# Scores one unit ahead of the attention, and seven pairs of query tiles by seven products instead of four

## The chip, the cores and the metric

The kernel runs on one core of a Trainium2 chip. The metric is the device time of one execution in microseconds (us); before the change it is 1146.06 us, the median of three runs (1145.57 to 1146.4). TensorE (PE in the profile) multiplies matrices, VectorE (DVE), ScalarE (ACT) and GpSimd (POOL) do elementwise work, and SyncE (SP) issues most DMAs. Each engine works through its own instructions in order.

## The reference, cut to what matters

Two layers on a sequence of 1024 positions with 1024 features, all in float32. The first is gated linear attention. The second, which the change touches, attends with eight query heads to one shared set of keys and values, in three groups of dilated windows (dilations 1, 4 and 16). It mixes the groups by their log-sum-exp, gates the result and projects it.

```python
q = rope(q.reshape(bsz, s, SWA_N_GROUPS * SWA_Q_HEADS, SWA_HEAD_DIM), pos) * (SWA_HEAD_DIM ** -0.5)
q = q.reshape(bsz, s, SWA_N_GROUPS, SWA_Q_HEADS, SWA_HEAD_DIM)
outs, lses = [], []
for gi, (window, dilation) in enumerate(SWA_GROUPS):
    o_g, lse_g = dilated_window_attention(q[:, :, gi], k_sh[:, :, gi], v_sh[:, :, gi], window, dilation)
    outs.append(o_g)
    lses.append(lse_g)
wts = jax.nn.softmax(jnp.stack(lses, axis=0), axis=0)
o = jnp.sum(wts[..., None] * jnp.stack(outs, axis=0), axis=0)
return (o.reshape(bsz, s, SWA_OUT).astype(x.dtype) * jax.nn.silu(g)) @ w_out
```

## The kernel before, in words

The program records its operations and then orders them itself: `Sched.order` (lines 263 to 405) is a list scheduler. Each operation has a cost from a table, `cost` (564 to 616), and a rank, the place where it was recorded, shifted by `S.later`. For each engine the scheduler takes, among the operations whose inputs and buffers are there, the one that can start first by these costs, and among equals the one recorded first. For TensorE an operand that comes from another engine counts 0.35 us later than it is expected (`AHEAD`). So the code's order of writing and the costs set the static order on each engine. All instructions are issued from line 462, which is why the profile names groups by tile and not by line.

Float32 products are made of three fast matmuls: high by high, high by low, low by high. The activations of the second layer lie in SBUF as `x1h` and `x1l`, the weights as `wh` and `wl`.

A unit is one query head with its three groups. For unit u, `q_proj` (1439) makes three query tiles of 128 features by 1024 positions: plain projections of 2 halves by 8 k-tiles by 3 matmuls into a bank `acc`, then a rotation (`rope`, 1227) on DVE, ACT and POOL. `g_proj` (1449) is a projection of the same size for the gate. `scores` (1466) multiplies Q by the keys in fp32 into two banks `lv`, takes the row minimum and the mask on DVE (statistics `sts` and `nat`), the exponential and its sum on ACT (tile `P`), then sends the statistics through DRAM (`std`, `nat<-std`), forms the weights of the groups on DVE (`cw`, `ew`) and sends these through DRAM too (`cwd`, `cw<-cwd`). `attend` (1552) scales P by the weights, makes the product of group 2 over a diagonal layout (`diag`, banks `po`), transposes P on TensorE (banks `ms`), forms `PT` on DVE and POOL, multiplies PT by V into `po` and adds into `og`.

Before the attention stands a stage in which pairs of 128-column tiles are projected by seven products instead of eight (`seven`, 1292): from sums of halves of the weights and of the activations (`T1` to `T4`, 16 pages). A product is 4 k-tiles by 3 matmuls of 512 columns. Its sums and combinations are extra passes on DVE, ACT and POOL. The three pairs of key tiles go this way, and the pairs of query tiles in the list `EARLY` (line 40), each entry two units and a group. These are rotated, stored to DRAM (`qd`) and loaded again by `q_proj` when their unit is due.

The loop of the attention (1646 to 1665) is: scores of u, gate of u-1, queries of u+1, attend of u. So projections of the units around stand between the scores and the attend of a unit. For unit 4 the keys and values change: `reload_k(1)` and `reload_v(1)` are recorded to wait for unit 3's weights (`S.behind(cwd[3])`). A pool of 16 pages `pg` holds K and V (three each), Q (three per unit) and part of P; smaller tiles share 13 buffers `a`.

Of the kernel before, what the change touches and what calls it, by code (L numbers as in the profile page):

```python
# [36 lines left out]
AHEAD = 0.35  # L37
RUNS, GATHER = 0.3, 1.0
QUEUED, ISSUE, ADDED = 2.4, 0.9, 1.7
EARLY = [(0, 1, 2), (2, 3, 2), (4, 5, 2), (6, 7, 2)]  # L40


class Buf:
# [100 lines left out]
class Sched:  # L144
# [21 lines left out]
    def record(self, engs, meth, args, kw):  # L166
# [17 lines left out]
        elif meth == "activation":  # L184
            func = str(a[2]).split(".")[-1]
        costs = [cost(e, meth, n, outs, ins, args, kw) + self.extra for e in engs]
        g = self.group_op
        if g is None:
# [355 lines left out]
def jump(v):  # L544

    i = v.idx.reshape(-1) if v.idx.ndim == 1 else v.idx[(0,) * 1]
    while i.ndim > 1 and i.shape[-1] == 1:
        i = i[..., 0]
    i = i.reshape(-1, i.shape[-1])[0] if i.ndim > 1 else i
    return int(abs(i[1] - i[0])) * SIZE[v.buf.dtype] if len(i) > 1 else 0  # L550
# [13 lines left out]
def cost(e, meth, n, outs, ins, args, kw):  # L564

    if e == "PE":
        if meth == "transpose":
            return 0.07
        n = int(_np.prod(outs[0].shape[1:]))
        fast = "float32r" in str(args[2].dtype)  # L570
        if fast:
            return n / 2400 + 0.0135 if n >= 256 else 0.215
        if n >= 128:
            return 4 * n / 2400 + 0.009
        if args[1].shape[0] == 64:
            return 0.12
        m = args[1].shape[1]
        return {32: 0.02, 64: 0.05}.get(m, 0.43)
    if meth == "dma_start":
        return 0.1 + int(_np.prod((outs + ins)[0].shape)) * 4 / 280e3  # L580
    psum = any(v.buf.pool.space == "PSUM" for v in ins)
    pointers = sum(isinstance(kw.get(k), View) for k in ("bias", "scale")) + 2 * (meth == "affine") + (meth == "scale")
    if e == "ACT":
        c = 0.105 + n * 0.83e-3 + 0.093 * pointers - 0.04 * psum
        if outs[0].dtype == U16:
            c += 0.09
        return c + (0.1 if "accum_out" in kw else 0)
    step = jump(outs[0]) if not psum or meth != "matmul" else 0
    if e == "DVE":
        if meth == "reciprocal":  # L590
            return 0.07 + n * 6e-3
        c = 0.07 + n / 960.0
        if meth in ("scalar_tensor_tensor", "tensor_tensor_reduce"):
            c += 0.06
        if meth in ("tensor_tensor", "tensor_mul", "tensor_add", "tensor_sub") and psum:
            c += 0.1
        if meth == "scalar_tensor_tensor" and psum:
            c += 0.05
        if meth == "tensor_tensor_scan":
            c += n / 960.0  # L600
        if meth in ("tensor_scalar", "scale") and not psum:
            c = 0.17 + n * 0.36e-3
        if meth == "affine":
            c = 0.2 + n * 0.52e-3
        if outs[0].dtype == U16:
            c += 0.04
        if step >= 2048 // 4 * 2:
            c += 0.75e-3 * n
        elif step >= 512:
            c += 2.2e-3 * n  # L610
        elif step >= 32 and n >= 256:
            c += 0.75e-3 * n
        return c + (0.085 if "accum_out" in kw else 0)
    if meth in ("tensor_scalar", "affine", "scale"):
        return 0.3 + n * 0.65e-3
    return 0.1 + n * 2.35e-3


def trunk(tc, xT, wP, wA, wA12, wAv3, w2, wO, wK, wV0, wV12, wB, wOB, par_d,
          ident_d, lmask_d, cos_d, sin_d, bmask_d, rmask_d, tri_d, lnr_d, out):  # L620
    S = Sched(tc, lat=LAT, pad=PAD)
# [18 lines left out]
    def page(pool, dt, name):  # L640
        return pool.tile([128, T], dt, name=name, tag="pg", bufs=16)
# [4 lines left out]
    def hs(half):  # L646
        return slice(half * 512, half * 512 + 512)
# [36 lines left out]
    def project(piece, xs, evac, halves=(0, 1), added=False):  # L684
        w = load_w(piece, added)
        for half in halves:
            acc = ps.tile([128, 512], F32, name="acc", bufs=2)
            proj_cols(w, xs, hs(half), acc)
            with S.later(-EVAC):
                evac(half, acc)  # L690
# [393 lines left out]
    def small(name, tag, bufs, dt=F32, shape=(128, 512)):  # L1084
        return hp.tile(list(shape), dt, name=name, tag=tag, bufs=bufs)
# [100 lines left out]
    vd0 = [dram.tile([128, T], F32, name=f"vd0{c}") for c in range(2)]  # L1186
    qd = {(u, g): dram.tile([128, T], F32, name=f"qd{u}{g}") for *us, g in EARLY for u in us}

# [4 lines left out]
    cwd = [dram.tile([2, T], F32, name=f"cwd{k}") for k in range(NK)]  # L1193
# [15 lines left out]
    def layer_b(xs, early):  # L1209
# [17 lines left out]
        def rope(pg, g, half, acc):  # L1227
            r = hs(half)
            t1 = small("t1", "t1", 2)
            S.vector.tensor_mul(t1, acc, cosT[:, r])  # L1230
            t2 = small("t2", "t2", 2)
            S.scalar.copy(t2[0:64, :], acc[64:128, :])
            S.scalar.copy(t2[64:128, :], acc[0:64, :])
            S.vp.tensor_mul(t2, t2, sinT[:, r])
            S.vp.tensor_add(to_group(pg, g, half), tok_view(t1, g), tok_view(t2, g))
# [141 lines left out]
        def load_v(c, g):  # L1377
            V[c][g] = page(p0, F32, f"V{c}{g}")
            if g == 1:
                for n in range(2):  # L1380
                    S.sync.dma_start(
                        V[c][g].rearrange("p (r n e) -> p r n e", r=4, n=2)[:, :, n, :],
                        vd[n * 512:n * 512 + 512, c * 128:c * 128 + 128].rearrange("(p r) e -> p r e", r=4))
            else:

                src = vd3[c].rearrange("(n a s k j) e -> k s a n (j e)", n=8, a=8, s=2, k=2)
                for k in range(2):
                    for s in range(2):
                        S.sync.dma_start(V[c][g][k * 64:k * 64 + 64, s * 512:s * 512 + 512], src[k, s])

        def sigmoid_gate(sg, acc):
            th = small("th", "t1", 2)
            S.scalar.activation(th, acc, AF.Tanh, scale=0.5)
            S.vector.scalar_tensor_tensor(sg, th, 1.0, acc, op0=OP.add, op1=OP.mult)
# [7 lines left out]
        jobs = [((wK[2 * g], kd[0][g]), (wK[2 * g + 1], kd[1][g]), g) for g in range(3)]  # L1402
        jobs += [((wB[u, g], qd[u, g]), (wB[v, g], qd[v, g]), g) for u, v, g in EARLY]
        w = load_pair([a[0] for a in jobs[0][:2]], True)
# [9 lines left out]
        def reload_k(c):  # L1414
            for g in (2, 1, 0):
                K[c][g] = page(p0, F32, f"K{c}{g}")
                S.sync.dma_start(K[c][g], kd[c][g])

        def reload_v(c):
            load_v(c, 2)  # L1420
            load_v(c, 1)
            V[c][0] = page(p0, F32, f"V{c}0")
            S.sync.dma_start(V[c][0], vd0[c])
# [15 lines left out]
        def q_proj(u):  # L1439
            Q = [page(p0, F32, "Q") for _ in range(3)]  # L1440
            U[u]["Q"] = Q
            for g in range(3):
                if (u, g) in qd:
                    S.sync.dma_start(Q[g], qd[u, g])
                else:
                    project(wB[u, g], xs, lambda half, acc: rope(Q[g], g, half, acc), added=True)


        def g_proj(u):
            og = U[u]["og"]  # L1450

            def evac(half, acc):
                sg, r = small("sg", "t2", 2), hs(half)
                sigmoid_gate(sg, acc)
                S.vector.scalar_tensor_tensor(og[:, r], og[:, r], 0.5, sg, op0=OP.mult, op1=OP.mult)
                if u < 6:
                    S.sync.dma_start(ogB[u][:, r], og[:, r])
            project(wB[u, 3], xs, evac, added=True)
# [184 lines left out]
            S.vp.memset(x, 0.0)  # L1643
        q_proj(0)
        reload_v(0)
        for u in range(8):
            scores(u)
            if 0 < u < 5:
                g_proj(u - 1)
            if u == 3:  # L1650
                with S.behind(cwd[3]):
                    reload_k(1)
            if u + 1 < 8:
                q_proj(u + 1)
            if u < 7:
                attend(u)
            if u == 3:
                with S.behind(cwd[3]):
                    reload_v(1)
        for u in (4, 5, 6):  # L1660
            g_proj(u)
        early()
# [59 lines left out]
    def early():  # L1722
        ogs.clear()
        for half in range(2):
            for kt in range(4):
                with S.later(-EVAC):
                    load_og(ogB[kt], kt, p0, lambda: small("ogf", "a", 13), (half,))

    U = layer_b(x1s, early)
    for half in range(2):  # L1730
        for kt in range(4, 6):
# [116 lines left out]
```

## Time and profile before

| what | value |
|---|---|
| median of 3 runs | 1146.06 us |
| profiled execution | 1145.4 us |
| its span | 1143.6 us |
| mean granted TensorE clock | 0.998 |
| busy, PE / DVE / ACT / POOL | 1129.4 / 813.4 / 583.9 / 181.7 us |
| seven-product stage | from about 511 to 640 us |
| attention, first score to last attend | from 664 to 1047 us |

The span is the time from the first to the last instruction; the profiled execution has 1.8 us around it. Matmul records overlap, since matmuls are pipelined: a 512-column matmul has a record of about 0.39 us, while the next starts 0.23 us later. So a mean of matmul records is not the price of one more matmul; the distance between starts is. "Idle before" names the engine or DMA that ended a wait. "PEld" is the loading of weights into TensorE, which runs beside the matmuls.

### The profile page before, as it was taken

The numbers are of one execution on the slowest core, as the hardware profiler recorded it, in microseconds if no ns is written. First come the engines' busy times: TensorE is split into PE (matmuls) and PEld (weight loads), VectorE is DVE, ScalarE is ACT, GpSimd is POOL, SyncE is SP. The second block draws the span as 40 slices with busy tenths as digits, with TensorE's granted clock in tenths as the row PEclk, the third lists the DMA queues.
The fourth block names the chain that finished last, engine by engine and source line by source line (L and its number), as shares of the span: only waits on it lengthen the run. The fifth ranks groups of instructions, "written<-read, shape, count | busy, mean of one in ns | idle before, by whom it ended". The sixth has DMA issues, their size and how long they took to land.

```text
span 1143.6 us, 20006 instructions
## 1 busy us (share of the span) xinstructions
PE 1129.4 (99%) x7696; PEld 959.8 (84%) x7696; DVE 813.4 (71%) x1634; ACT 583.9 (51%) x1165; POOL 181.7 (16%) x168
## 2 busy tenths in 40 slices
PE   9999999999999999999999999999999999999997
PEld 9888888889987888887888878888878888888886
DVE  6286963686967599988989556676656667587578
ACT  5355531545563345656566467355545655643242
POOL 1000000100222111022232212022120122133000
PEclk9999999999999999999999999999999999999999
DMA  8111122211253453865566863444273433462545
GB/s 270 59 39 38 64 85 74 93 57 38 75 173 113 138 169 135 283 200 133 136 176 164 235 152 77 94 84 99 59 177 86 93 81 71 97 146 77 171 143 180
DMA packets 104031, 138.29 MB, mean 121 GB/s; under 512 B 44833, under 2 KB 63137, under 8 KB 103937
## 3 DMA queue, kind: packets, MB, share of 16 engines
q1 hardware_dynamic: 97888, 119.72, 34.2%
q0 software_dynamic: 6048, 17.30, 8.6%
q8 instruction: 60, 0.98, 0.3%
q14 instruction: 35, 0.28, 0.1%
HBM read 109.53 MB, written 27.46 MB: 120 GB/s over the span
## 4 chain that ended last, share of the span: by engine, by line
PE 89%; DVE 7%; ACT 1%; DMA 1%; issue 1%; SPq 0%; DVEq 0%; ACTq 0%
PE acc L462 47%; PE sev L462 11%; PE lv L462 9%; PE po L462 9%; PE vac L462 7%; PE ms L462 4%; PE pro L462 2%; DVE rt L462 2%; DVE wl L462 1%; DMA nat<-std 1%; DVE x1l L462 1%; DVE t L462 1%; DVE P L462 1%; ACT t L462 0%; DVE Q L462 0%
## 5 line engine op out<-in xcount | busy, mean ns | idle before, releaser
L462 ACT ACTIVATE wh<-wf 128x1024 fp32r<-128x1024 f32 (+3 forms) x111 | 106.4, 960 | 158.3 <-PE acc L462 118.3
L462 PE MATMUL acc<-x1h,wh 128*128 128x512 f32 x384 | 165.6, 431 | 1.0 <-ACT t L462 1.0
L462 PE MATMUL acc<-x1h,wl 128*128 128x512 f32 x384 | 150.6, 392 | 0.0
L462 PE MATMUL acc<-x1l,wh 128*128 128x512 f32 x384 | 150.0, 391 | 0.0
L462 DVE TENSOR_TENSOR wl<-wf,wh 128x1024 fp32r<-128x1024 f32 (+3 forms) x62 | 76.7, 1237 | 43.9 <-ACT wh L462 33.7
L462 PE MATMUL acc<-xh,wh 128*128 128x512 f32 x256 | 102.1, 399 | 0.0
L462 PE MATMUL acc<-xh,wl 128*128 128x512 f32 x256 | 99.9, 390 | 0.0
L462 PE MATMUL acc<-xl,wh 128*128 128x512 f32 x256 | 99.9, 390 | 0.0
L462 ACT ACTIVATE P<-P,sts 128x256 f32<-128x256 f32 (+1 forms) x128 | 59.9, 469 | 65.9 <-DVE sts L462 65.3
L462 PEld LDWEIGHTS acc<-x1h,wl 128*128 128x128 f32 x384 | 72.1, 188 | 15.9
L462 PEld LDWEIGHTS acc<-x1h,wh 128*128 128x128 f32 x384 | 72.6, 189 | 13.0 <-ACT t L462 1.2
L462 PEld LDWEIGHTS acc<-x1l,wh 128*128 128x128 f32 x384 | 72.6, 189 | 12.0
L462 PE MATMUL lv<-K,Q 128*64 128x64 f32 (+2 forms) x512 | 71.1, 288 | 0.9 <-DVE sts L462 0.8
L462 PE MATMUL sev<-T,wh 128*128 128x512 f32 x224 | 69.3, 391 | 0.1
L462 POOL DMA_DIRECT2D wl<-in_wB x36 | 31.8, 903 | 225.6 <-ACT wl L462 177.3
L462 DVE CUSTOM_DVE_ANT_0 P<-lv,bmask 128x256 f32<-128x256 f32 (+1 forms) x128 | 46.2, 378 | 27.4 <-PE lv L462 26.8
L462 PEld LDWEIGHTS lv<-K,Q 128*128 128x128 f32 (+1 forms) x512 | 53.8, 164 | 12.6 <-DVE sts L462 2.6
L462 PE MATMUL acc<-ogh,wh 128*128 128x512 f32 x152 | 60.3, 397 | 0.1
L462 PE MATMUL acc<-ogl,wh 128*128 128x512 f32 x152 | 59.4, 391 | 0.2 <-POOL ogl L462 0.2
L462 PE MATMUL acc<-ogh,wl 128*128 128x512 f32 x152 | 59.3, 390 | 0.0
L462 DVE TENSOR_TENSOR t<-t,sinT 128x512 f32<-128x512 f32 x46 | 34.4, 748 | 33.7 <-ACT t L462 33.6
L462 POOL TENSOR_TENSOR wl<-wf,wh 128x1024 fp32r<-128x1024 f32 x8 | 19.1, 2386 | 240.3 <-PE ms L462 145.5
(298 smaller groups left out, 2839.1 us busy)
## 6 DMA issues: line engine op xcount, KB each, us to landing
wf<-in_wB SPq DMA_DIRECT2D x32, 512.0 KB
wf<-in_wA SPq DMA_DIRECT2D x24, 512.0 KB
wl<-in_wB POOLq DMA_DIRECT2D x24, 512.0 KB, 7.9
wf<-in_wO SPq DMA_DIRECT2D x16, 512.0 KB
wf<-in_wOB SPq DMA_DIRECT2D x16, 512.0 KB
wf<-in_wV SPq DMA_DIRECT2D x12, 512.0 KB
res<-in_xT SPq DMA_DIRECT2D x16, 256.0 KB
x1d<-rt SPq DMA_DIRECT2D x16, 256.0 KB
```

The lines of the kernel that those rows point to most:

```text
L462: getattr(handle[o.eng], meth)(*[conv(a) for a in args], **{k: conv(v) for k, v in kw.items()})
```

## The change

`EARLY` gets three more entries: the group-1 query tiles of units 1 and 3, of 4 and 5, and of 6 and 7 are made as pairs by seven products before the attention, and stored to DRAM. Only group 0 of every unit, and group 1 of units 0 and 2, are still projected inside the attention. The table's cost of a transpose on TensorE goes from 0.07 to 0.11, which can move instructions everywhere in the program.

The loop is rewritten: scores of unit 0 and queries of unit 1 come first; then, for each u, scores of u+1, gate of u-1, queries of u+2, attend of u. So the P tiles of two units are held at once. The keys of the second half are loaded ahead of the scores of unit 4, still behind unit 3's weights; its values are no longer held behind those.

```diff
-EARLY = [(0, 1, 2), (2, 3, 2), (4, 5, 2), (6, 7, 2)]
+EARLY = [(0, 1, 2), (2, 3, 2), (1, 3, 1), (4, 5, 2), (6, 7, 2), (4, 5, 1), (6, 7, 1)]
...
         if meth == "transpose":
-            return 0.07
+            return 0.11
...
-        for u in range(8):
-            scores(u)
-            if 0 < u < 5:
-                g_proj(u - 1)
+        scores(0)
+        q_proj(1)
+        for u in range(7):
             if u == 3:
                 with S.behind(cwd[3]):
                     reload_k(1)
-            if u + 1 < 8:
-                q_proj(u + 1)
-            if u < 7:
-                attend(u)
+            scores(u + 1)
+            if 0 < u < 5:
+                g_proj(u - 1)
+            if u + 2 < 8:
+                q_proj(u + 2)
+            attend(u)
             if u == 3:
-                with S.behind(cwd[3]):
-                    reload_v(1)
+                reload_v(1)
```

## The prediction

> **What bounds the kernel now.** First the page: one engine fills the span.
>
> ```profile
> span 1143.6 us, 20006 instructions
> PE 1129.4 (99%) x7696; PEld 959.8 (84%) x7696; DVE 813.4 (71%) x1634; ACT 583.9 (51%) x1165; POOL 181.7 (16%) x168
> ```
>
> TensorE shows 99%, and the next engine, VectorE, 71%. Then the windows, for the two stages that the change touches: the seven-product stage, and the attention from the first score matmul to the last attend.
>
> ```profile
> 664.15:1047.00 382.85, 379.08 (x2273) 324.71 (x2273) 255.78 (x806) 214.74 (x616) 79.95 (x89) 1.00 0.44 96
> 518.00:640.00 122.00, 121.82 (x537) 100.96 (x538) 103.08 (x142) 75.16 (x126) 36.57 (x34) 1.00 0.63 168
> ```
>
> The columns behind the length are PE, PEld, DVE, ACT, POOL, then the granted clock and the DMA share. PE idles 382.85 - 379.08 = 3.8 us in the attention and 0.2 us in the other. So in both the time is the PE's work, and a matmul less is its slot less, as long as the other engines keep up. How long a slot is stands in the chain that ended last:
>
> ```profile
> 518.18 122.24 PE sev L462 x538
> 640.42 23.80 PE acc L462 x105
> ```
>
> 122.24/538 = 0.2272 us for a 512-column matmul of the seven-product stage, 23.80/105 = 0.2267 us for one of a plain projection.
>
> **Part 1: fewer matmuls.** A plain query tile costs 2 halves x 8 k-tiles x 3 = 96/2 = 48 matmuls, a pair 96. By seven products a pair costs 7 x 4 x 3 = 84. Three more pairs: 3 x 12 = 36 matmuls fewer, 36 x 0.227 = **-8.2 us**. The rest of a pair's price is on other engines (four sums, their splits, five combining adds, about 13 passes on DVE or POOL); at 103.08 of 122.00 us DVE has room in that stage, and three more pairs repeat the same mix, so this costs nothing. Without that cover it would cost what DVE needs beyond PE, and DVE needs 0.85 of it. The group-1 store of a rotated half has a strided output, but so have those of the K pairs and group-2 pairs that run there already:
>
> ```profile
> L462 DVE TENSOR_TENSOR pair<-t,t 128x512 f32<-128x512 f32 x28 | 29.4, 1049 | 2.4 <-DMA qd<-pair 1.2 <-POOL t L462 0.5
> qd<-pair SPq DMA_DIRECT2D x8, 512.0 KB
> wl<-in_wB POOLq DMA_DIRECT2D x24, 512.0 KB, 7.9
> ```
>
> On the queues, six 512 KB reads with add on POOL's queue become nine of 256 KB, and SP gets six more 512 KB stores to qd and six more loads of Q. At a DMA share of 0.63 and 0.44 these lie beside PE work: nothing.
>
> **Part 2: fewer changes of kind.** In the attention, projection matmuls are pushed between fp32 matmuls (scores, transposes, P times V). Here is what a change costs on PE (start, length):
>
> ```profile
> 670.35 0.38 PE L462 MATMUL lv<-K,Q 128*128 128x128 f32 x2
> 670.49 0.48 PE L462 MATMUL acc<-x1h,wh 128*128 128x512 f32 x1
> 670.80 0.40 PE L462 MATMUL acc<-x1l,wh 128*128 128x512 f32 x1
> 671.03 0.40 PE L462 MATMUL acc<-x1h,wl 128*128 128x512 f32 x1
> 671.27 0.59 PE L462 MATMUL lv<-K,Q 128*128 128x256 f32 x2
> 671.51 0.58 PE L462 MATMUL acc<-x1h,wh 128*128 128x512 f32 x1
> 671.93 0.40 PE L462 MATMUL acc<-x1l,wh 128*128 128x512 f32 x1
> ```
>
> The first projection matmul behind a score takes 0.31 and 0.42 us to the next start instead of 0.23. Over the kernel, the matmul that stands first in each group of three is longer than the second:
>
> ```profile
> L462 PE MATMUL acc<-x1h,wh 128*128 128x512 f32 x384 | 165.6, 431 | 1.0 <-ACT t L462 1.0
> L462 PE MATMUL acc<-x1l,wh 128*128 128x512 f32 x384 | 150.0, 391 | 0.0
> ```
>
> 165.6 - 150.0 = 15.6 us. The order of before has 121 such changes in the attention, that of after 106: 15.6/121 = 0.129 us each, 15 x 0.129 = **-1.9 us**. Both ends: nothing, if the longer matmuls come from another cause, and -1.9.
>
> **Part 3: waits in the attention.** The projection matmuls that fill it fall from 1047 to 756, and the order there changes. TensorE, unit 2's diagonal product in before (po<-diag is the group-2 product, ms the transposes of P, lv the next scores):
>
> ```order
> L462 MATMUL acc<-x1h_4386,wh 128x512
> L462 MATMUL acc<-x1l_4399,wh 128x512
> L462 MATMUL acc<-x1h_4386,wl 128x512
> L462 MATMUL acc<-x1h_4412,wh 128x512
> L462 MATMUL acc<-x1l_4426,wh 128x512
> L462 MATMUL acc<-x1h_4412,wl 128x512
> L462 MATMUL po<-diag,V_6513 128x128 x8
> L462 MATMUL acc<-x1h_4437,wh 128x512
> L462 MATMUL acc<-x1l_4452,wh 128x512
> L462 MATMUL acc<-x1h_4437,wl 128x512
> L462 MATMUL lv<-K_6281,Q 128x256
> ```
>
> TensorE in after, attend(1) into scores(3):
>
> ```order
> L462 MATMUL acc<-x1h_4335,wl 128x512
> L462 MATMUL ms<-ident,P 128x128 x4
> L462 MATMUL po<-diag,V_7020 128x128 x8
> L462 MATMUL ms<-ident,P 128x128 x8
> L462 MATMUL lv<-K_6780,Q 64x64 x16
> L462 MATMUL po<-PT,V_7027 128x128 x12
> L462 MATMUL po<-PT,V_7033 128x128
> L462 MATMUL lv<-K_6788,Q 128x128
> L462 MATMUL acc<-x1h_4366,wh 128x512
> L462 MATMUL acc<-x1l_4377,wh 128x512
> L462 MATMUL acc<-x1h_4366,wl 128x512
> L462 MATMUL po<-PT,V_7033 128x128 x14
> ```
>
> The attend now runs as one block with almost no projection between its steps. Before has one bare place of this kind, and it waits (timeline of PE; the bracket is the idle time ahead):
>
> ```profile
> 842.44 0.60 PE L462 MATMUL ms<-ident,P 128*128 128x128 f32 x4
> 844.08 2.21 PE L462 MATMUL po<-diag,V 128*128 128x128 f32 x16 [1.04 <-DVE diag L462]
> 847.32 0.51 PE L462 MATMUL acc<-x1h,wh 128*128 128x512 f32 x1 [1.03 <-ACT t L462]
> ```
>
> 1.04 + 1.03 = 2.07 us. In after the diagonal product is not so bare: in attend(1) eight transposes and twelve projections precede the four shown, the first four being its own. I take one such double wait more, +2.1; the ends are -3.8 (all idle gone) and seven times 2.07.
>
> The second place is on VectorE, whose in-order queue holds the reduction that waits for a unit's gathered statistics (cw<-nat). In before it stands among the rotations of the next Q:
>
> ```order
> L462 TENSOR_TENSOR Q<-t_7654,t_7656 128x512
> L462 TENSOR_TENSOR t_7701<-acc,cosT 128x512
> L462 TENSOR_REDUCE cw<-nat 128x8
> L462 TENSOR_TENSOR ew<-cw,nat 128x24
> L462 TENSOR_TENSOR t_7712<-t_7712,sinT 128x512
> L462 TENSOR_TENSOR Q<-t_7701,t_7712 128x512
> ```
>
> In after, VectorE in attend(5), with unit 6's statistics (PT are the transposed P, nat and sts unit 7's statistics):
>
> ```order
> L462 TENSOR_TENSOR PT<-ms,upto 128x512
> L462 COPY_PREDICATED PT<-below,ms 128x512
> L462 TENSOR_TENSOR og<-po,og 128x512
> L462 ISA P,nat<-lv,rmask 128x64
> L462 ISA nat 128x1
> L462 ISA P,nat<-lv,rmask 128x64
> L462 ISA nat 128x1
> L462 ISA P,sts<-lv,bmask 128x128
> L462 ISA sts 128x1
> L462 TENSOR_REDUCE cw<-nat 128x8
> L462 TENSOR_TENSOR ew<-cw,nat 128x24
> L462 TENSOR_TENSOR og<-po,og 128x512
> ```
>
> Behind it wait the add that frees the po banks and unit 7's score reductions, for which PE waits. How long the gather takes when it binds, in the chain:
>
> ```profile
> 664.22 1.50 PE lv L462 x34
> ...
> 842.61 0.45 PE ms L462 x4
> ...
> 861.02 3.12 PE po L462 x28
> ...
> 882.24 0.45 PE lv L462 x2
> ...
> 883.60 2.45 DMA std<-sts
> ...
> 888.69 6.82 DMA nat<-std
> 895.52 0.20 DVE cw L462
> ```
>
> From the second store to the reduction 895.52 - 883.60 = 11.9 us. In after PE has, between unit 6's last score and that place, 3 projections 0.7, the diagonal 2.2, 12 transposes 1.4, the 64-wide scores 1.5 and 19 products of P with V (3.12/14 each) 4.2: 10.0 us, less 883.60 - 882.24 = 1.4 until the store: 8.6 of cover. Late by 0 to 3.3 us; I take the middle, +1.7. In the other units the same sum is larger (at least 24 more projections, 5.4 us, stand there), so I cost those at nothing. The new K for unit 4, loaded behind unit 3's weights, has 96 projections (21.8 us) and two attends ahead of its first score: nothing.
>
> **Sum.** -8.2 - 1.9 + 2.1 + 1.7 = -6.3. The profiled execution took 1145.4 us (span 1143.6 and 1.8 around it), 0.7 under the median of 1146.06: 1139.1 for its like, **1139.8** for the median.
>
> A rule that would cut the gain: the Trainium skill, page "TensorE: Matmul & The Clock Gate", section "Back-to-back issue gap", gives about 131 ns per 512-column matmul sustained in a stream with weight loads; by it part 1 would be an estimated 4.7 us and the time 1143.3. The trace disagrees: 0.227 us over 538 of them.
>
> **The rivals.** *Bare attends wait often.* Four more units pay the 2.07 us of the place at 842: -10.1 + 8.3 = -1.8, 1144.3, no change. For it: seven attends are packed now; against: eight transposes and the 64-wide scores stand in the gaps. Chance 0.16.
>
> *The gather holds VectorE* (slower). Its place is the reduction among the PT steps, in units 1, 2, 3, 5 and 6. If each comes 3.3 us late, 5 x 3.3 = 16.5: 1146.06 - 10.1 + 16.5 = 1152.5. It decides from 10.1/5 = 2.0 us per unit. For it: 11.9 us has been seen, and everything behind is needed by PE; against: the DMA share there is 0.44, and the cover is over 10 us but for unit 6. Chance 0.11.
>
> *A matmul out frees only its weight load.* The change would then do less than it says:
>
> ```profile
> L462 PEld LDWEIGHTS acc<-x1l,wh 128*128 128x128 f32 x384 | 72.6, 189 | 12.0
> ```
>
> 36 x 0.189 = 6.8 instead of 8.2: 1141.2. Against it stands the 0.227 between starts. The shorter slot of the Trainium skill's page named above points the same way. Chance 0.03.
>
> **How the numbers follow.** The forecast has 0.70, with a range of its own from 1132.2 (-8.2 - 1.9 - 3.8) to 1143.6 (the two waits half as long again, and the changes of kind worth nothing: -8.2 + 5.7). The 80% range goes from 1133 to 1147: it takes in the packed attends and leaves out most of the gather case. A measurement of this kernel tells 0.2% (2.3 us) from no change. Faster: 0.70 + 0.03 = 0.73; within it 0.16; slower 0.11.
>
> **What would show it.** The chain's seven-product stretch should hold 252 matmuls more (three pairs of 84) at 0.227; the attention should be near 382.85 - 291 x 0.2267 - 1.9 + 3.8 = 319 us, with PE idle near 7 to 8. Waits of PE for diag or PT summing over 8 us would show the first rival; a wait of DVE cw for the DMA over 10 us the second. If the stage of sevens shows PE idle for DVE, part 1 is wrong.

## The result, and the profile after

The changed kernel takes 1139.95 us, the median of five runs (1136.77 to 1141.5), against 1146.06 us (1145.43 to 1146.99) before. The ratio is 0.9944, with a 95% interval of 0.9925 to 0.9963: faster by 6.1 us. The forecast was 1139.8. The total is right, but the experiments show that two of its steps are not: waits of 3.8 us in the attention that didn't come, and no term for the new price of a transpose, which costs 7.8 us. That these errors cancel is luck. One execution, the profiled one of the kernel e7_wldve below, took 2899.84 us and is left out of that kernel's median.

The page of after, its first two lines:

```profile
span 1137.9 us, 20061 instructions
PE 1122.0 (99%) x7660; PEld 953.9 (84%) x7660; DVE 838.2 (74%) x1663; ACT 590.0 (52%) x1183; POOL 190.3 (17%) x187
```

36 matmuls fewer (7696 to 7660), and TensorE still fills the span. The windows of after, for the attention, for the seven-product stage, and for ten microseconds ahead of both (columns as before: the length, busy PE, PEld, DVE, ACT, POOL, then the granted clock and the DMA share):

```profile
725.91:1041.20 315.29, 313.26 (x1990) 271.26 (x1990) 227.63 (x762) 188.30 (x580) 70.94 (x93) 1.00 0.45 107
518.00:702.00 184.00, 182.50 (x805) 150.75 (x804) 156.36 (x214) 112.37 (x190) 54.45 (x50) 1.00 0.60 162
478.00:488.00 10.00, 7.66 (x30) 5.99 (x29) 6.47 (x9) 2.70 (x4) 1.53 (x1) 0.83 0.81 240
```

In the attention PE idles 315.29 - 313.26 = 2.0 us, where before had 3.8 and the forecast wanted 7 to 8. In the stage of sevens it idles 1.5 us instead of 0.2. The third row shows 2.3 us of idle time in 10 and a granted clock of 0.83. In before the longest single wait of PE is 1.04 us, and the clock stays at 1.00 up to the last matmul.

The waits of PE and PEld in the attention of after (in total, times, longest):

```profile
PEld lv L462 <- DVE sts L462: 2.1, 4, 0.9
...
PEld po L462 <- DVE diag L462: 1.3, 1, 1.3
...
PEld po L462 <- DVE PT L462: 0.9, 2, 0.6
...
PE po L462 <- DVE diag L462: 0.8, 1, 0.8
```

They are all small. The stretches of the profiled executions, from the starts of their matmuls, show where the time went. The last column is the kernel with the change but with the old price of a transpose, which comes up below.

| stretch, us (in brackets PE's idle time between its first and last matmul) | before | after | after, price 0.07 |
|---|---|---|---|
| up to the first product of the value projection | 432.4 (0.4) | 432.6 (0.5) | 432.7 (0.4) |
| from there to the last of the seven-product stage | 207.7 (1.6) | 269.3 (4.8) | 265.1 (1.9) |
| from there to the first score | 24.1 | 24.1 | 24.1 |
| attention and what follows | 479.5 (3.8) | 411.9 (2.1) | 408.9 (0.8) |
| span | 1143.6 | 1137.9 | 1130.7 |

With the old price the second stretch grows by 57.4 us, which is 252 x 0.228: the three pairs at their slot and nothing else. In after it grows by 61.6. The extra 4.2 us are waits and a slower clock ahead of the attention. The timeline of PE in after shows the larger part (start, length, operation, idle time ahead):

```profile
478.10 0.39 PE L462 MATMUL vac<-wh,x1l 128*128 128x512 f32 x1
480.83 0.84 PE L462 MATMUL ms<-ident,rt 128*128 128x128 f32 x4 [2.34 <-DVE x1r L462]
...
481.89 0.63 PE L462 MATMUL vac<-wl,x1h 128*128 128x512 f32 x1
482.31 0.63 PE L462 MATMUL vac<-wh,x1l 128*128 128x512 f32 x1
...
484.45 0.43 PE L462 MATMUL vac<-wl,x1h 128*128 128x512 f32 x1
484.72 0.39 PE L462 MATMUL vac<-wh,x1l 128*128 128x512 f32 x1
```

Four transposes of the first layer's result wait 2.34 us for VectorE. Behind the wait a matmul starts every 0.43 us instead of every 0.23, until 484.4. The trace has the granted clock at 0.5 for 3.41 us there, which costs half of that, 1.7 us. What VectorE did meanwhile, and POOL beside it, stands in two timelines of after:

```profile
476.61 3.46 DVE L462 TENSOR_TENSOR x1l<-rt,x1h 128x512 fp32r<-128x512 f32 x2
480.00 0.68 DVE L462 COPY x1r<-ms 128x512 f32<-128x512 f32 x1
```

```profile
476.94 2.59 POOL L462 TENSOR_TENSOR wl<-wf,wh 128x1024 fp32r<-128x1024 f32 x1 [5.25 <-ACT wh L462]
```

Two subtractions take 3.46 us while POOL subtracts weights. The second wait stands in the stage of sevens: PE waits 1.50 us until 540.05, for ACT, and the chain goes back to a weight load:

```profile
527.72 8.47 DMA wf<-in_wK
536.34 1.73 POOL sum L462
538.09 0.63 ACT wh L462
538.75 0.63 ACT t L462
539.40 0.61 ACT u L462
540.05 162.14 PE sev L462 x714
```

### The profile page after: what moved, and what is told of

It is laid out like the page before. It is cut to its first block, busy times and chain, and to the rows that moved or that the text cites. A ratio compares the mean times of both kernels' runs of the same rounds, so it can differ in the third digit from the quotient of the medians.

```text
span 1137.9 us, 20061 instructions
## 1 busy us (share of the span) xinstructions
PE 1122.0 (99%) x7660; PEld 953.9 (84%) x7660; DVE 838.2 (74%) x1663; ACT 590.0 (52%) x1183; POOL 190.3 (17%) x187
## 4 chain that ended last, share of the span: by engine, by line
PE 84%; DVE 8%; DMA 3%; ACT 2%; issue 1%; POOL 0%; SPq 0%; DVEq 0%; ACTq 0%; POOLq 0%
PE acc L462 41%; PE sev L462 15%; PE po L462 9%; PE lv L462 8%; PE vac L462 5%; PE ms L462 3%; PE pro L462 3%; DVE rt L462 2%; DVE wl L462 1%; DMA wf<-in_wOB 1%; DVE x1l L462 1%; DVE P L462 1%; DMA wf<-in_wK 1%; ACT wh L462 1%; DMA ogf<-ogB 1%
## 5 line engine op out<-in xcount | busy, mean ns | idle before, releaser
L462 PE MATMUL acc<-x1h,wh 128*128 128x512 f32 x288 | 126.7, 440 | 0.0
L462 PE MATMUL acc<-x1h,wl 128*128 128x512 f32 x288 | 113.0, 392 | 0.0
L462 PE MATMUL acc<-x1l,wh 128*128 128x512 f32 x288 | 112.4, 390 | 0.0
L462 PE MATMUL sev<-T,wh 128*128 128x512 f32 x320 | 98.9, 389 | 0.5 <-DVE T L462 0.5
L462 PEld LDWEIGHTS sev<-T,wh 128*128 128x128 f32 x320 | 60.0, 188 | 13.3 <-DVE T L462 0.9
L462 POOL DMA_DIRECT2D wl<-in_wB x39 | 34.5, 909 | 192.8 <-ACT wl L462 174.5
L462 PEld LDWEIGHTS acc<-x1h,wl 128*128 128x128 f32 x288 | 54.0, 188 | 12.0
L462 PEld LDWEIGHTS lv<-K,Q 128*128 128x128 f32 (+1 forms) x512 | 53.6, 163 | 11.9 <-DVE sts L462 2.1
L462 PE MATMUL sev<-T,wl 128*128 128x512 f32 x160 | 62.3, 389 | 0.0
L462 PEld LDWEIGHTS acc<-x1l,wh 128*128 128x128 f32 x288 | 54.4, 189 | 8.7
L462 PEld LDWEIGHTS acc<-x1h,wh 128*128 128x128 f32 x288 | 54.3, 189 | 8.6
```

The source lines that it names most:

```text
L462: getattr(handle[o.eng], meth)(*[conv(a) for a in args], **{k: conv(v) for k, v in kw.items()})
```

## The experiments

Two theories stood after this. **A**: the gain is the matmuls, and the new price of a transpose (0.11 for 0.07), which the prediction did not cost, reorders the work ahead of the attention and gives part of it back. **B**: the new waits come from the pairs themselves. A third, **C**, came with the loop: how much projection work is left to cover the attention's waits decides. (In the expectation of e3_loop, C is the stronger claim that the loop alone gives the gain.) All times are medians against before in runs on the same chip; ratios have 95% intervals.

| kernel | pairs | loop | price | median, us | ratio to before |
|---|---|---|---|---|---|
| after | 7 | new | 0.11 | 1139.95 | 0.9944 (0.9925 to 0.9963) |
| e1_t07 | 7 | new | 0.07 | 1132.11 | 0.9878 (0.9863 to 0.9893) |
| e2_t11 | 4 | old | 0.11 | 1151.52 | 1.0046 (1.0034 to 1.0059) |
| e3_loop | 4 | new | 0.07 | 1144.09 | 0.9984 (0.9976 to 0.9993) |
| e4_pairs | 7 | old | 0.07 | 1157.9 | 1.0102 (1.0088 to 1.0116) |
| e6_t11att | 7 | new | 0.11 for P only | 1137.16 | 0.993 (0.9918 to 0.9942) |
| e6b_t11rest | 7 | new | 0.11 for all but P | 1134.25 | 0.9894 (0.9876 to 0.9911) |
| e7_wldve | 7 | new | 0.11 | 1138.5 | 0.9942 (0.993 to 0.9954) |
| e9_six07 | 6 | new | 0.07 | 1134.12 | 0.9897 (0.9883 to 0.9912) |
| e5b_eight07 | 8 | new | 0.07 | 1144.98 | 0.9996 (0.9987 to 1.0004) |
| e10_qdve | 8 | new | 0.07 | 1137.16 | 0.9933 (0.9916 to 0.9949) |
| e8_ten07 | 10 | new | 0.07 | 1170.83 | 1.0211 (1.0193 to 1.0229) |

### The price alone, taken out and put in

In after the price goes back; in before the same line goes the other way, from 0.07 to 0.11:

```diff
-            return 0.11
+            return 0.07
```

> The changed kernel with the table's price of a transpose back at 0.07, pairs and loop as changed. Theory A (the gain is the 36 matmuls; the new price alone reordered VectorE and GpSimd ahead of the attention, which there makes TensorE wait 2.5 us at 478 us and run at half clock for 3.4 us behind it): about 4 us of the 4.7 us lost ahead of the attention come back, near 1136. Theory B (the waits ahead of the attention come from the pairs themselves, longer stage and more loads): no change, near 1140.

> The kernel before with the price of a transpose at 0.11 alone. Theory A: it gets the same wait and half clock ahead of the attention and nothing in return but fewer changes of kind (103 instead of 121, 2.3 us): 1147 to 1149. Theory B: no loss ahead of the attention, 1144 to 1146.

Without the price the change gives 13.7 us (1145.8 to 1132.1), more than A gave it; the price alone costs before 5.7 us, where A expected 1 to 3. B falls: the wait at 478 stands in before with the new price too (here in e2_t11's timeline), and not in after with the old one.

```profile
481.56 0.82 PE L462 MATMUL ms<-ident,rt 128*128 128x128 f32 x4 [2.30 <-DVE x1r L462]
```

e1_t07 is faster than both before and after. Its attention, in the windows, and its waits of PE there:

```profile
721.87:1036.50 314.63, 313.88 (x1997) 272.62 (x1997) 226.31 (x760) 186.48 (x574) 82.25 (x104) 1.00 0.47 108
```

```profile
PE lv L462 <- DVE sts L462: 0.4, 1, 0.4
PE po L462 <- DVE diag L462: 0.2, 1, 0.2
```

PE idles 0.75 us in 314.6. The two waits that the prediction put into this stage (3.8 us) are not there.

### The loop alone, the pairs alone

e3_loop is after with the price 0.07 and the short list; e4_pairs is before with the long list:

```diff
 # e3_loop, against after
-EARLY = [(0, 1, 2), (2, 3, 2), (1, 3, 1), (4, 5, 2), (6, 7, 2), (4, 5, 1), (6, 7, 1)]
+EARLY = [(0, 1, 2), (2, 3, 2), (4, 5, 2), (6, 7, 2)]
 # and 0.11 becomes 0.07
```

> Four pairs as before, price 0.07, with the new loop alone. Theory A: only changes of kind (101 instead of 121, 20 x 0.13 = 2.6 us) and some of the 3.8 us of idle time in the attention: 1142 to 1144. Theory C (the loop, not the pairs, gives the gain): near 1140.

> Seven pairs, price 0.07, with the old loop. Theory A: 8.2 us for the matmuls and 1.0 for eight changes of kind less, with waits as in before: near 1137. Theory C (without the new loop the attend lacks projections to cover its waits): the attention waits more, 1142 or above.

The loop alone saves 1.7 us (its interval, 0.9976 to 0.9993, leaves out 1). That is near A's 1142 to 1144 and not the 1140 of a gain that the loop gives alone. The pairs alone cost 12.1 us. Together they save 13.7. The attention of e4_pairs, and the waits of PE in it:

```profile
720.91:1068.05 347.14, 329.13 (x2034) 278.90 (x2034) 232.36 (x770) 190.98 (x586) 66.24 (x82) 1.00 0.42 99
```

```profile
PE acc L462 <- DVE sg L462: 4.3, 2, 3.1
PE po L462 <- DVE PT L462: 3.4, 3, 2.2
PE ms L462 <- DVE P L462: 3.0, 2, 2.3
PE lv L462 <- DVE sts L462: 2.6, 4, 1.5
```

PE idles 18.0 us. With the old loop the attention's own chains (statistics, P, PT) had been covered by the projections that the pairs take away; with the scores a unit ahead, 0.75 us of idle time is left on the same list. So the 8.2 us of matmuls come from the pairs, and the loop is what lets them through. A and its 1137 fall here, C holds. The idle time is most of it and not all: against e1_t07 the span is 23.5 us longer, the attention idles 17.3 us more, and where the other 6 lie was not found.

Ahead of two of e4_pairs' longer waits (2.31 us at 882.95, 1.53 us at 939.74) stands a small operation of VectorE that takes seven times as long as elsewhere, beside an addition on POOL:

```profile
879.66 1.28 DVE L462 TENSOR_TENSOR ew<-cw,nat 128x24 f32<-128x24 f32 x1
```

```profile
879.61 1.28 POOL L462 TENSOR_TENSOR Q<-t,t 128x512 f32<-128x512 f32 x1 [0.64 <-DVE t L462]
```

Such pairings stand in the covered orders too: a product of VectorE takes 2.18 us beside POOL's Q in before (917.87), and 1.88 us in e1_t07 (738.36), yet the next waits of PE are only 0.34 and 0.43 us. So what a pairing costs seems to depend on the cover; no run here takes the two apart.

### Which transposes' price

The price applies to the transposes of P in the attention and to others ahead of it.

```diff
-            return 0.11
+            return 0.11 if args[1].buf.name == "P" else 0.07   # e6_t11att
+            return 0.07 if args[1].buf.name == "P" else 0.11   # e6b_t11rest
```

> The changed kernel with the price 0.11 for the transposes of P in the attention alone, 0.07 for all others: ahead of the attention the order is that of the kernel before, in the attention nearly that of the changed kernel. Theory A: of the 7.8 us that the price costs, the 4.2 us lost between 432 and 702 us come back and the 3.1 us lost in the attention and behind it stay: 1135 to 1136. Theory D (the price of the transposes in the attention does the harm, the wait at 478 us is hidden anyway): near 1140.

> The complement: price 0.11 for all transposes but those of P in the attention, which have 0.07. Theory A: the wait at 478 us, the half clock and the wait at 538 us are there, 4.2 us, and the attention is that of 0.07: 1132.1 + 4.2, near 1136. Theory D (the attention's price does the harm): near 1132.

The two prices act apart: e6b_t11rest has after's order up to the attention and e1_t07's from there on, e6_t11att the reverse. For P the price costs 5.0 us (1137.16 - 1132.11). For the others it costs 2.1, and there the intervals of e6b_t11rest and e1_t07 overlap; the wait ahead of the attention is in its profile, with 2.31 us. Both results lie between what A (4.2 us lost ahead of the attention, 3.1 in it and behind it) and D (the attention alone) expected: both places have a part, and by the medians the attention's is the larger. In the attention the idle time of the order with 0.11 was 2.0 us in the profiled execution of after, 3.4 in e6_t11att and 5.0 in e7b_look (below), and 0.75 in both kernels with the other order. One place differs among the three: the same eight products of PT with V start without a wait at 1000.86 in after, wait 1.48 us in e6_t11att and 3.14 us in e7b_look. The chain of e7b_look shows what they wait for:

```profile
987.09 8.57 DMA ogf<-ogB
...
997.36 0.69 DVE ogl L462
998.05 1.03 DVE P L462 x3
999.08 0.34 DVE PT L462
...
999.46 1.17 PE po L462 x8
```

The 0.11 order has put a split of the first layer's output (`ogl`) ahead of P and PT in VectorE's queue, and that split waits for a load whose time varies (7.46 us in the chain of e6_t11att, 8.57 us here). This explains part of the 5 us and can explain part of the wider spread (4.7 us from the fastest to the slowest run of after, 1.0 in e1_t07). The idle time of after's attention and of what follows is 1.4 us above e1_t07's, of a difference of 3.1; where the other 1.7 us lie was not found.

### The weight split off POOL

The split of the value projection's weights, which ran on POOL at 476.94, is put on VectorE; TensorE's order stays as in after.

```diff
-    def split_lo(dst, src, hi):
-        S.vp.tensor_sub(dst, src, hi.bitcast(F32))
+    def split_lo(dst, src, hi, eng=None):
+        (eng or S.vp).tensor_sub(dst, src, hi.bitcast(F32))
...
-                wh, wl = load_w(wV12[:, k0:k0 + 2, :])
+                wh, wl = load_w(wV12[:, k0:k0 + 2, :], False, S.vector)
```

> The changed kernel with the low parts of the V projection's weights split on VectorE alone, never on GpSimd; TensorE's order is unchanged. Theory A (a 2.6 us subtraction on GpSimd holds VectorE's two-input subtraction beside it for as long, TensorE waits 2.3 us for the copy behind that and then runs at half clock for 3.4 us): the wait at 478 us and the half clock go, 1.1 us, and the wait of 1.7 us at 538 us, which stands at another operation, may stay: 1136 to 1139. Theory E (the wait belongs to TensorE's own order, a transpose of four blocks placed too early): wait and half clock stay, 1140.

> One more look at the changed kernel with the V projection's low weights split on VectorE alone, for its stages. Theory A: no wait of over 1 us between 432 and 505 us, no half clock there, that stage 72.4 us long as in the kernel before; the wait at 538 us stays, so the stage of sevens stays near 195 us. Theory E: the wait of about 2.4 us and the half clock for 3.4 us stay, the stage is 73.5 us.

The kernel's stages are read from e7b_look, a second profile of the same kernel (one execution, 1140.6 us). VectorE in e7b_look, at the same place:

```profile
477.19 1.29 DVE L462 TENSOR_TENSOR x1l<-rt,x1h 128x512 fp32r<-128x512 f32 x2
478.39 0.68 DVE L462 COPY x1r<-ms 128x512 f32<-128x512 f32 x1
479.00 1.22 DVE L462 TENSOR_TENSOR wl<-wf,wh 128x1024 fp32r<-128x1024 f32 x1
```

The same two subtractions take 1.29 us instead of 3.46, and on VectorE the split itself takes 1.22 instead of 2.59. The wait at 478 and the half clock behind it are gone, and the stretch up to the last of the sevens is 264.1 us instead of 269.3. So the cause of the wait is shown: POOL's subtraction beside VectorE's, with TensorE's order unchanged. E (the wait belongs to PE's own order) falls. The wait at 540, which was expected to stay, went too: the load of `wf` ahead of it took 7.05 us there instead of 8.47. Yet the median is 1138.5, not told apart from after's 1139.95: in the execution of e7b_look the wait of 3.14 us at 999 and a half clock behind it took back what the front gave. Whether that is so in the other executions, the runs don't say.

### One pair less, one more, three more

e9_six07 is e1_t07 without `(1, 3, 1)`; e5b_eight07 has one more entry, e8_ten07 three:

```diff
-EARLY = [(0, 1, 2), (2, 3, 2), (1, 3, 1), (4, 5, 2), (6, 7, 2), (4, 5, 1), (6, 7, 1)]
+EARLY = [(0, 1, 2), (2, 3, 2), (1, 3, 1), (4, 5, 2), (6, 7, 2), (4, 5, 1), (6, 7, 1),
+         (0, 2, 1), (2, 3, 0), (4, 5, 0)]   # e5b_eight07: only the first of these three
```

> Price 0.07, new loop, six pairs (without units 1 and 3, group 1). Theory A: each covered pair is worth 12 matmuls, 2.7 us, give or take a microsecond of waits and changes of kind: 1132.1 + 2.7, 1134 to 1136. Theory C (what a pair does is set by the cover of the attention, and seven hits a lucky order): no steady step, 1139 or above, or no worse than 1132.

> Price 0.07, new loop, an eighth pair (units 0 and 2, group 1). Theory A: 12 matmuls fewer, 2.7 us, and 11 changes of kind fewer, 1.4 us, against seven pairs at 0.07 (1132.1): near 1128. Theory C (the attention runs out of projections that cover its waits): 1132 or above, with over 3 us of idle TensorE in the attention.

> Price 0.07, new loop, ten pairs (also group 0 of units 2 and 3 and of 4 and 5). Theory A: 36 matmuls fewer, 8.2 us, and 33 changes of kind fewer, 4.3 us, against seven pairs at 0.07: near 1120. Theory C: 495 projection matmuls in the attention instead of 765 no longer cover it; 10 to 20 us of waits as with seven pairs and the old loop, 1130 or above.

From six to seven pairs the time falls by 2.0 us, near the 2.7 of twelve matmuls, as A had it (the executions of the two kernels lie apart, the intervals of their ratios overlap). The eighth pair costs 12.9 us, and ten cost 38.7 against seven, as C had it. The projections left in the attention, counted in the traces, are 855, 759, 654 and 495 for six, seven, eight and ten pairs (the expectations have 765 and 669 for seven and eight), and the idle time of PE there is 0.6, 0.75, 9.6 and 27.2 us. In these orders the cover ends between 759 and 654. The longest wait with ten pairs, in e8_ten07's windows and on its PE and ACT:

```profile
814.90:822.60 7.70, 0.36 (x4) 0.17 (x2) 3.12 (x11) 3.64 (x13) 0.80 (x1) 0.86 0.95 219
```

```profile
822.72 1.97 PE L462 MATMUL ms<-ident,P 128*128 128x128 f32 x8 [7.46 <-ACT P L462]
```

```profile
819.59 1.31 ACT L462 ACTIVATE P<-P,cw 128x256 f32<-128x256 f32 x3 [2.52 <-DMA cw<-cwd]
822.26 1.20 ACT L462 ACTIVATE P<-P,cw 128x128 f32<-128x128 f32 x3 [1.37 <-DMA cw<-cwd]
```

P can't be scaled until the weights of the groups are back from DRAM, with the DMA engines 0.95 busy. This is the gather of the prediction's slower rival, by its second trip rather than its first, and three pairs further on.

With eight pairs something else comes in, the collision that e4_pairs shows too. VectorE and POOL in e5b_eight07, ahead of a wait of 1.95 us:

```profile
775.90 0.18 DVE L462 TENSOR_REDUCE cw<-nat 128x8 f32<-128x24 f32 x1
776.11 0.20 DVE L462 RECIPROCAL cw<-cw 128x8 f32<-128x8 f32 x1
776.35 1.48 DVE L462 TENSOR_TENSOR ew<-ew,cw 128x24 f32<-128x24 f32 x1
```

```profile
776.22 1.57 POOL L462 TENSOR_TENSOR Q<-t,t 128x512 f32<-128x512 f32 x1
```

A product of 24 columns, 0.18 us elsewhere, takes 1.48: it ends at 777.83, when POOL's addition ends (777.79). The scores' row minima stand behind it. The last run puts that addition on VectorE:

```diff
-            S.vp.tensor_add(to_group(pg, g, half), tok_view(t1, g), tok_view(t2, g))
+            S.vector.tensor_add(to_group(pg, g, half), tok_view(t1, g), tok_view(t2, g))
```

> Eight pairs, the transpose price 0.07, and the last addition of a rotation (Q<-t,t) always on VectorE. With eight pairs the attention had 9.6 us of TensorE's idle time and two spells of half clock; ahead of the 1.95 us wait at 778 VectorE's 0.18 us product ew took 1.48 us while POOL's Q<-t,t ran for 1.57 us, and ahead of the 2.04 us wait at 818 VectorE's t took 3.00 us beside POOL's P and Q. Theory F (the two engines block one another, and that is what the eighth pair ran into): with Q off POOL these two waits and the half clock behind them go, 2 + 2 + 3.4 us: 1136 to 1140 us, idle in the attention under 6 us. Theory C (669 projections are too few to cover the attention's chains whichever engine adds): the waits come back elsewhere, idle 8 us or more, 1142 us or more. The edit also moves the planner's order in the attention, so a result between the two decides nothing.

The waits of PE in the attention, of e5b_eight07 and then of e10_qdve:

```profile
PE lv L462 <- DVE sts L462: 6.6, 6, 2.0
PE acc L462 <- ACT t L462: 2.4, 1, 2.4
```

```profile
PE acc L462 <- ACT t L462: 2.4, 1, 2.4
PE lv L462 <- DVE sts L462: 1.4, 4, 0.6
```

1137.16 us, 7.8 less, as F had it: the waits for the statistics fall from 6.6 to 1.4 us, no half clock is left, and the idle time of the attention is 5.3 us. The edit also moved the planner's order, so F is supported and not isolated. It is still 5 us slower than seven pairs with the old price, so the cover seems too thin as well.

## Why the prediction was right, and where it wasn't

**What bounds it.** Right: PE 99% again, and every difference found is matmuls, PE's idle time, or its clock.

**Part 1, -8.2.** Right in size: 252 matmuls more at 57.4/252 = 0.228 us in the stage of sevens (e1_t07), and one covered pair measured at 2.0 us (six to seven) against 2.7. That DVE has room was right too: 156.36/184.00 = 0.85, as before. "Nothing" for the pairs' other work held with the price 0.07. The wait of 1.50 us in the stage of sevens is not the sign against this part that the prediction named (PE idle for DVE): ACT ends it, it goes back to a weight load, and it is not there with that price. What it left out is that the price of the matmuls taken away depends on the cover of the attention: with the old loop the same three pairs cost 12.1 us.

**Part 2, -1.9.** Right in kind, a little large: the two groups on which it rests, in after:

```profile
L462 PE MATMUL acc<-x1h,wh 128*128 128x512 f32 x288 | 126.7, 440 | 0.0
L462 PE MATMUL acc<-x1l,wh 128*128 128x512 f32 x288 | 112.4, 390 | 0.0
```

126.7 - 112.4 = 14.3 instead of 15.6: -1.3 us, for about the 106 changes that were counted.

**Part 3, +3.8.** Wrong in sign. "One such double wait more" became one wait of 0.8 us for the diagonal product, and VectorE's reduction `cw` waits for no DMA in the attention. The idle time fell by 1.7 us instead. The step that failed is that a place in the order was priced by the wait of a place that looks like it: at 842 in before nothing stands between the diagonal product and the four transposes (842.44) that it depends on, so PE waits while VectorE copies the diagonal. In after other matmuls stand there: in attend(1) twelve projections and four transposes, and no wait; nine projections at the one place that still waits (781.80). For unit 6 the 11.9 us of one gather were set against a cover of 8.6; in after 8.7 us pass from that unit's last pair of stores (issued at 965.88) to its first reduction (974.59), and VectorE is busy up to it, so the gather took no longer than that, and the cover was enough.

**The price of a transpose** has no term at all in the sum. It is the largest error in the sum: it costs 7.8 us in the medians (after against e1_t07), 5.7 on before. Of 7.1 us between the two profiled spans, 4.3 are idle time and 1.7 the half clock.

**The sum.** In the profiled executions: matmuls -8.2, changes of kind -1.3, idle time over the whole span +1.6 (5.8 to 7.3 us), half clock +1.7: -6.2, against 1137.9 - 1143.6 = -5.7. The forecast's -6.3 had +3.8 of waits in the attention that didn't come, and lacked the waits ahead of it that did.

**The rivals.** The bare attends don't wait in after. The gather holds nothing in it; its mechanism is real, and stands behind the longest wait with ten pairs. That a matmul out frees only its weight load falls with 0.228.

## What to carry to other kernels

A number in a planner's cost table is a change of its own: here 0.04 us on one operation undid more than half of what the rest of the change gave (7.8 of 13.7 us), so time each part of a combined change alone and together, as pairs and loop were worth +12.1 and -1.7 us apart and -13.7 together. Work taken out of a stage pays nearly its full slot as long as what is left covers the chains of the other engines, and then it can cost several times that at once: 2.0 us gained by the seventh pair, 12.9 lost by the eighth (of which 7.8 came back with one addition moved off POOL). When a small operation of VectorE is suddenly five times as long, look at what POOL runs at that moment before looking at dependencies.

## What the runs showed of the hardware

**VectorE and POOL.** Subtractions of two SBUF operands on VectorE took 3.46 us for two beside a subtraction of two SBUF operands on POOL (after), and 1.29 us without (e7b_look); a product of 24 columns took 1.48 us instead of 0.18. The Trainium skill, page "SBUF — State Buffer", section "Who interferes with whom", states that a VectorE instruction with two SBUF inputs contends with a GpSimd instruction that reads SBUF, over a shared read port. The traces agree: the 24-column product ends with POOL's addition.

**The clock.** The granted clock fell to 0.5 for 3.41 us behind waits of PE of 2.34 us (after) and 3.14 us (e7b_look), and twice in e5b_eight07, behind 1.95 and 2.04 us. In the windows of that kernel:

```profile
775.70:783.00 7.30, 5.35 (x19) 3.29 (x17) 6.31 (x24) 5.91 (x26) 2.08 (x2) 0.77 0.86 153
```

It did not fall behind the same wait of 2.31 us in the profiled execution of e6b_t11rest, nor behind 3.07 us in e4_pairs, nor behind 2.37 us in e5b_eight07 itself. So it is no fixed length of idle time. Executions of one kernel differ in it too: those of after at a mean clock of 0.998 took 1136.77 and 1138.48 us, those at 0.996 and 0.997 took 1139.95 to 1141.5. The Trainium skill, page "TensorE: Matmul & The Clock Gate", section "Why this matters for your kernels", advises against idle gaps of more than about 3 us; here 2 us were enough in some executions. What decides between them stays open.
